# Scaling both halves of the recurrence's array, and splitting the streamed weights, on VectorE in place of GpSimd

## The chip, the cores and the metric

The kernel runs on one core of one Trainium2 chip. The metric is the device time of one execution in microseconds (us), lower is better. Five engines work side by side, each through its own queue in order: TensorE (PE in the rows; its weight loads are PEld), VectorE (DVE), ScalarE (ACT), GpSimd (POOL) and SyncE (SP), which issues nearly all DMAs. They wait for one another through semaphores.

## What is computed

One layer of a diffusion backbone on 1280 tokens: 1024 latent tokens and 256 prompt tokens, 1024 channels. It is a SwiGLU feed-forward (ffn1), a token-mixing step, and a second feed-forward (ffn2). All products have single-precision accuracy. Cut to the token mixing, which the change is about:

```python
proj = h @ p['w_mix_in']
hq, hi, hf_fwd, hf_bwd, hg, aq, ak, av = jnp.split(proj, idx, axis=-1)

def forget(hf):
    f = lb_h + (1.0 - lb_h) * jax.nn.sigmoid(heads(hf, DK_A).astype(jnp.float32))
    return jnp.log(f), 1.0 - f

lf_f, k_f = forget(hf_fwd)
lf_b, k_b = forget(hf_bwd)
o_f, s_f = hgrn_scan(q_rec, k_f, lf_f, i_rec, s0_f)
o_b, s_b = hgrn_scan(rev(q_rec), rev(k_b), rev(lf_b), rev(i_rec), s0_b)
o_rec = rms_norm(o_f + rev(o_b), p['hgrn_out_norm']).astype(h.dtype) * jax.nn.silu(heads(hg, DV_A))
...
o = jnp.concatenate([o_rec.reshape(B, T, -1), o_att.reshape(B, T, -1)], axis=-1) @ p['w_mix_out']
```

`hgrn_scan` is a gated linear recurrence of four heads, in both directions: the state is multiplied by f and gains k times v at each token; the output reads it with q.

## The kernel before

**Products in two parts.** A single-precision product is made of three reduced ones: each factor is split into a high part (a cast, tile name ending in h) and a low part (the factor minus its high part, ending in l), and `mm3` adds high×high, high×low and low×high. Activations are split once and stay in the on-chip memory (`hh`, `hl`). Weights come from HBM in pieces of 128x1024: `rload` (line 91) issues the DMA into a raw tile, `wload` (line 99) lets ACT cast the high part and one more engine subtract to get the low part. That engine is DVE while `self.half` is set, which is so in the prompt half of each feed-forward's first product, and POOL at all other times. `ahead(n)` keeps n pieces ready; four high and four low tiles go round. Pieces that POOL splits: the first two of ffn1, 32 of the input projection (`w_mix_in`), 24 of the output projection (`w_mix_out`), and the first three of ffn2, 61 in all.

**The recurrence of one head** (`hgrn`, from line 1060 on, with `hgrn_in` before it). All 1280 tokens stand in the free dimension. `A` holds k of both directions, `B` holds q times f of both, `P` (variable `pr`) the products of f over blocks. First `I` is the sum of A's two directions and a masked product (`sd`) fills the diagonal of the scores `s64`. Then come seven levels of doubling block size s: PE multiplies a rearranged copy of A (`I`, made by ACT) with B (40 small matmuls, tile `h0s` for head 0), DVE puts the result into `s64` under a mask (two `COPY_PREDICATED`), DVE multiplies one half of A (1280 columns) by block products, and B's two half arrays (640 columns each) are multiplied by block products in place: the one at offset 0 by DVE, the one at offset NT+s by POOL. POOL then makes the next level's `P` by multiplying neighbours. The next level's PE products need both halves of B and the new `I`.

**What runs beside it.** The generator of the recurrence is stepped by `tick` after every half of a projection's bank (24 matmuls of 256 columns), so PE alternates 24 projection matmuls with the 40 small ones of a level. The projection beside a head differs: head 0 and head 2 run the gate `hg` and a key or query projection, head 1 the values and keys, head 3 the second query group first. For the gate, POOL multiplies a 128x512 tile by the norm's gain (`hg<-hg,gam`) after each bank; for queries and keys DVE and POOL share the norm and the rotary embedding.

**Order.** Within an engine the order is not the source order: a scheduler at build time lists what is ready on its own clock, by program order among the ready. In the attention PE, DVE and ACT are pinned to the source order. At run time each queue is in order.

Of the kernel before, what the change touches and what calls it, by code (L numbers as in the profile page):

```python
# [9 lines left out]
F32 = mybir.dt.float32  # L10
# [3 lines left out]
ALU = mybir.AluOpType  # L14
# [8 lines left out]
NT = NS + NP  # L23
# [10 lines left out]
def sub(a, off, dims):  # L34
    return bass.AP(tensor=a.tensor, offset=a.offset + off,
                   ap=[list(a.ap[0])] + [list(d) for d in dims])


class Engine:


    def __init__(self, tc, eng):
        self.tc, self.eng, self.pinned = tc, eng, False
# [22 lines left out]
class Kern:  # L66
    def __init__(self, tc, ins, outs):
        self.tc, self.nc, self.i, self.o = tc, Engines(tc), ins, outs
        self.wq, self.wready, self.side = deque(), deque(), []
        self.h, self.hgen = [None] * 3, [None] * 3  # L70
        self.nw, self.nblk, self.half, self.tb = 0, 0, False, 7
        self.acc, self.nsq, self.ops, self.xt = [{}, {}, {}], [0] * 3, {}, [None] * 3
        self.late, self.lgen = deque(), None
        self.rawq, self.xraw, self.nraw, self.nr = deque(), None, 1, 0
# [24 lines left out]
    def wload(self):  # L99
        nc = self.nc  # L100
        if not self.rawq:
            self.rload()
        raw, name = self.rawq.popleft()
        shape = list(raw.shape)
        hi = self.wp.tile(shape, F32R, tag="wh", bufs=4, name=name + "h")
        nc.scalar.copy(hi, raw)
        lo = self.wp.tile(shape, F32R, tag="wl", bufs=4, name=name + "l")
        self.nw += 1
        eng = nc.vector if self.half else nc.gpsimd
        eng.tensor_tensor(lo, raw, hi.bitcast(F32), op=ALU.subtract)  # L110
        self.wready.append((hi, lo))
        while len(self.rawq) < self.nraw and self.wq:
            self.rload()
# [945 lines left out]
    def hgrn(self, ap, gp, hd, arrs):  # L1059
        nc = self.nc  # L1060
        A, B, q, pr = arrs
# [10 lines left out]
        def interleave(s):  # L1072
            I = gp.tile([P, NT], F32, tag="I", bufs=2, name=f"{n_}I{s}")
            nc.scalar.copy(I.rearrange("p (c r j) -> p c r j", r=2, j=s),
                           sub(A, 0, [(2 * s, NT // (2 * s)), (NT + s, 2), (1, s)]))
            return I

        def pairs(I, lv, move):


            banks = []
            for a, e in ((0, 8), (8, 10)):
                b = self.bank(f"{n_}s{lv}_{a}", (e - a) * 64)
                for t in range(a, e):
                    for h in range(2):
                        nc.tensor.matmul(b[64 * h:64 * h + 64, (t - a) * 64:(t - a + 1) * 64],
                                         I[:, t * P + 64 * h:t * P + 64 * h + 64], move(t * P, h), start=True, stop=True,
                                         tile_position=(0, 64 * h))
                banks.append((a, e, b.rearrange("p (a b) -> p a b", b=64)))
            return banks  # L1090
# [6 lines left out]
        s = 1  # L1097
        for lv in range(7):
            nb = NT // s
            C = nb // 2  # L1100
            if lv < 6:
                banks = pairs(I, s, lambda o, h: sub(B, o + 64 * h, [(2 * s, 32 // s), (NT + s, 2), (1, s)]))
            else:
                banks = pairs(I, s, lambda o, h: sub(B, o + (1 - h) * (NT + 64), [(1, 64)]))
            v_a = sub(A, 0, [(NT + s, 2), (2 * s, C), (1, s)])
            nc.vector.tensor_tensor(v_a, v_a, sub(pr, 1, [(nb - 1, 2), (2, C), (0, s)]), op=ALU.mult)
            if lv < 6:
                I = interleave(2 * s)
            for eng, off, po in ((nc.vector, 0, nb + 1), (nc.gpsimd, NT + s, 0)):
                v_b = sub(B, off, [(2 * s, C), (1, s)])  # L1110
                eng.tensor_tensor(v_b, v_b, sub(pr, po, [(2, C), (0, s)]), op=ALU.mult)
            for a, e, b in banks:
                if lv < 6:
                    nc.vector.copy_predicated(s64[:, a:e], self.mask[:, lv].unsqueeze(1).to_broadcast([P, e - a, 64]), b)
                else:
                    for h in range(2):
                        r = slice(64 * h, 64 * h + 64)
                        nc.scalar.copy(sc[r, a:e, 64 - 64 * h:128 - 64 * h], b[r])
            if lv == 6:
                for h in range(2):  # L1120
                    r = slice(64 * h, 64 * h + 64)
                    nc.scalar.copy(sc[r, :, 64 * h:64 * h + 64], s64[r])
            p2 = gp.tile([P, nb], F32, tag="P2" if lv % 2 == 0 else "P1", name=f"{n_}P{2 * s}")
            nc.gpsimd.tensor_tensor(p2, sub(pr, 0, [(2, nb)]), sub(pr, 1, [(2, nb)]), op=ALU.mult)
            pr = p2
            s *= 2
            if lv < 6:
                yield
# [387 lines left out]
def build(tc, ins, outs):  # L1516
    K = Kern(tc, ins, outs)
    nc = K.nc
# [11 lines left out]
    def ffn(st, name, which, hp, xp, side, nxt, done):  # L1530

        win, wout = ins[f"w_{name}_in"], ins[f"w_{name}_out"]
        pool = {}
        ai, pi = K.stream(K.in_blocks(win, name, lambda: pool["fp"]))
        ao, po = K.stream(K.out_blocks(wout, name, hp, xp, lambda: pool["op"]))
        ap_, pp = K.stream(K.prompt_out_blocks(wout, name, lambda: pool["op"]))

        def after():
            K.out_resident(hp, wout, name)
            ao(2)  # L1540
        K.half = True
        K.xraw, K.nraw = st["raw"](), 3
        K.prompt_in(st["t"], name)
        K.finish_all()
        K.half = False
        K.xraw, K.nraw = None, 1
        ai(1)
        st["close"]()
        with K.pool(name + "fp", side=side) as fp:
            pool["fp"] = fp  # L1550
            st["side"]()
            K.latents_in(fp, name, pi, after)
            K.finish_all()
        st["end"]()
        with K.pool(name + "op", side=side) as op:
            pool["op"] = op
            K.tb = 8
            m = 3 * which + 2
            K.latents_out(name, po, K.mt[m], K.ng[m], lambda c, d: done(op, c, d), lambda: ap_(2))
            K.prompt_out(name, pp, K.mt[m], lambda c, d: done(op, c, d))  # L1560
            nxt(op)

    with ExitStack() as top:
# [9 lines left out]
        with K.pool("xx", side="right") as xp:  # L1573
# [61 lines left out]
            def nxt(op):  # L1635
                mix_units()
                K.ahead(2)
                ap = pv.enter_context(K.pool("pv"))
                K.att_consts(cp, ap)
                K.proj_v(ap, 0)  # L1640
                K.finish_all()
                pv.close()
            ffn({"t": qp, "raw": lambda: qp, "close": q1.close, "side": lambda: K.side.append(adas()), "end": ta.close},
                "ffn1", 0, hp, xp, "right", nxt, done1)
        K.tb = 7
# [56 lines left out]
        with K.pool("xx2") as xp:  # L1702
# [29 lines left out]
            with K.pool("ps2", PSUM) as p:  # L1732
                K.ps = p, 8
                for c in (2, 1):
                    K.mix_out(c, range(8), done2)

                def done3(op, c, d):
                    K.nsq[c] += 1
                    if K.nsq[c] == 4:
                        K.nsq[c] = 0  # L1740
                        K.side.append(K.out_y(op, c, d // 4))
                ffn({"t": qp, "raw": lambda: hq["p"], "close": q1.close, "side": lambda: None, "end": lambda: None},
                    "ffn2", 2, hp, xp, None, lambda op: K.finish_all(), done3)
# [42 lines left out]
```

## Time and profile before

| | |
|---|---|
| median of 3 runs | 2743.75 us (2738.01, 2743.75, 2744.55) |
| the profiled execution | 2738.21 us, of which the span from first to last instruction is 2736.4 us |
| PE busy | 2658.0 us, 97% of the span |
| DVE busy | 1716.5 us, 63% |
| ACT busy | 1118.4 us, 41% |
| POOL busy | 861.5 us, 31% |
| mean granted TensorE clock | 0.991 of full speed |

In all profile rows times are microseconds from the span's start unless marked ns, `x` is a count of instructions, `out<-in` names the written and read tiles (buffer numbers left out), and `L49` is the line of a helper through which every operation is recorded. A timeline row is: start, duration, engine, line, operation, tiles, shape, count, and in brackets the idle time of that engine just before and what ended it. An instruction's duration runs from when its queue takes it up; a wait inside the engine counts as duration.

### The profile page before, as it was taken

How to read it: one execution, taken by the hardware profiler on the slowest of the kernel's cores; microseconds unless marked ns; L12 is line 12 of the kernel's file. 1: busy time of each engine (PE TensorE's matmuls, PEld its weight loads, DVE VectorE, ACT ScalarE, POOL GpSimd, SP SyncE). 2: the span in 40 equal slices, each digit the busy share in tenths (PEclk: the TensorE clock that was granted, in tenths of full speed). 3: DMA queues.
4: the chain of work that ended last, by engine and by line, in shares of the span. 5: the costliest groups of instructions: out<-in, count | busy, mean ns of one | idle time of the engine just before them, and what ended most of it. 6: DMA issues, size and time to landing. Idle time of an engine off the chain costs nothing.

```text
span 2736.4 us, 43768 instructions
## 1 busy us (share of the span) xinstructions
PE 2658.0 (97%) x17070; PEld 2330.0 (85%) x17070; DVE 1716.5 (63%) x2416; ACT 1118.4 (41%) x1896; POOL 861.5 (31%) x644
## 2 busy tenths in 40 slices
PE   7999999999998999999989899999999999999999
PEld 6987777888887989898989788888988888888889
DVE  4965454657978445555564588757855555658865
ACT  5732222323446423232322577735632333334444
POOL 1034444440002346556553121154034444420000
PEclk8999999999999999999999999999999999999999
DMA  9965665328645532232314845385743233358455
GB/s 313 275 181 185 191 191 185 101 97 304 211 138 182 171 97 78 86 100 67 95 57 144 194 106 119 137 267 166 210 137 110 91 108 105 107 173 291 137 179 191
DMA packets 412244, 429.29 MB, mean 157 GB/s; under 512 B 20620, under 2 KB 314756, under 8 KB 409988
## 3 DMA queue, kind: packets, MB, share of 16 engines
q1 hardware_dynamic: 411856, 426.43, 50.2%
q8 instruction: 134, 2.20, 0.3%
q14 instruction: 74, 0.61, 0.1%
q10 hardware_dynamic: 180, 0.06, 0.0%
HBM read 326.79 MB, written 99.61 MB: 156 GB/s over the span
## 4 chain that ended last, share of the span: by engine, by line
PE 58%; DVE 5%; POOL 2%; DMA 1%; issue 1%; ACT 0%; SPq 0%; POOLq 0%; DVEq 0%; ACTq 0%
PE ffn2po L49 8%; PE mob L49 4%; PE ffn2pp L49 2%; PE ffn2pg L49 2%; PE ffn2pu L49 2%; PE ffn1pp L49 1%; PE hi0b L49 1%; PE aq0b L49 1%; PE ak0b L49 1%; PE ak1b L49 1%; PE av1b L49 1%; PE hg1b L49 1%; PE hg0b L49 1%; PE hi1b L49 1%; PE ffn2u10p L49 1%
## 5 line engine op out<-in xcount | busy, mean ns | idle before, releaser
L49 POOL TENSOR_TENSOR nr<-nm,nh 128x4 f32<-128x4 f32 (+1 forms) x9 | 9.0, 1005 | 275.8 <-DVE nm L49 275.8
L49 PE MATMUL ffn1pp<-ffn1pvv,ffn1pw 128*128 128x256 f32 x528 | 65.5, 285 | 5.3 <-DVE ffn1pvv L49 5.3
L49 PEld LDWEIGHTS ffn1pp<-ffn1pvv,ffn1pw 128*128 128x128 f32 x528 | 63.9, 192 | 6.7 <-DVE ffn1pvv L49 6.1
L49 PE MATMUL ffn2pp<-ffn2pvv,ffn2pw 128*128 128x256 f32 x528 | 64.0, 283 | 0.0
L49 PEld LDWEIGHTS ffn2pp<-ffn2pvv,ffn2pw 128*128 128x128 f32 x528 | 63.6, 192 | 0.1
L49 DVE TENSOR_TENSOR sacc<-sacc,sq 128x512 f32<-128x512 f32 (+1 forms) x36 | 44.7, 1251 | 12.8 <-ACT sq L49 12.5
L49 POOL TENSOR_TENSOR hl<-nt,hh 128x256 fp32r<-128x256 f32 (+1 forms) x20 | 23.2, 1160 | 62.5 <-ACT hh L49 62.5
L49 POOL TENSOR_TENSOR ffn2w00a<-ffn2r,ffn2w00a 128x512 fp32r<-128x512 f32 x3 | 3.9, 1284 | 122.3 <-ACT ffn2w00a L49 122.3
L49 DVE TENSOR_TENSOR ffn1pw<-ffn1pw,ffn1pw 128x512 fp32r<-128x512 f32 x44 | 34.5, 813 | 7.9 <-ACT ffn1pw L49 7.9
L49 DVE TENSOR_TENSOR ffn2pw<-ffn2pw,ffn2pw 128x512 fp32r<-128x512 f32 x44 | 30.0, 690 | 13.7 <-ACT ffn2pw L49 12.1
L49 POOL TENSOR_TENSOR ffn1w00a<-ffn1r,ffn1w00a 128x512 fp32r<-128x512 f32 x3 | 3.9, 1292 | 107.3 <-ACT ffn1w00a L49 107.3
L49 ACT ACTIVATE nt<-nt,mt,sv 128x256 f32<-128x256 f32 (+1 forms) x40 | 25.8, 681 | 25.7 <-DVE sv L49 15.4
L49 ACT CAST ffn2pw<-ffn2pw 128x512 fp32r<-128x512 f32 x44 | 26.9, 619 | 16.0 <-PE ffn2pp L49 7.6
L49 ACT CAST ffn1pw<-ffn1pw 128x512 fp32r<-128x512 f32 x44 | 25.5, 616 | 14.8 <-DMA ffn1pw<-w_ffn_out 8.8
L49 PE MATMUL ada<-wada,cst 128*32 128x256 f32 x448 | 30.0, 385 | 0.0
L49 DVE TENSOR_REDUCE a_0mx<-a_0S 128x1 f32<-128x1536 f32 x8 | 14.1, 1757 | 24.6 <-DMA a0k<-k_d 13.2
L49 PEld LDWEIGHTS ada<-wada,cst 128*32 128x32 f32 x448 | 11.7, 109 | 14.7 <-issue 9.9
L49 PE MATMUL ffn1po<-ffn1w_10g,ffn1w_10b 128*128 128x512 f32 x84 | 20.6, 394 | 0.0
L49 PE MATMUL ffn2po<-ffn2w_4g,ffn2w_4b 128*128 128x512 f32 x84 | 20.4, 391 | 0.0
L49 PE MATMUL ffn2po<-ffn2w_5g,ffn2w_5b 128*128 128x512 f32 x84 | 20.4, 391 | 0.0
L49 PE MATMUL ffn1po<-ffn1w_8g,ffn1w_8b 128*128 128x512 f32 x84 | 20.3, 391 | 0.0
L49 PE MATMUL ffn2po<-ffn2w_6g,ffn2w_6b 128*128 128x512 f32 x84 | 20.3, 390 | 0.0
(4079 smaller groups left out, 9951.8 us busy)
## 6 DMA issues: line engine op xcount, KB each, us to landing
wada<-w_ada SPq DMA_DIRECT2D x112, 256.0 KB, 4.3
ffn1r<-w_ffn_in SPq DMA_DIRECT2D x44, 512.0 KB, 4.0
ffn2r<-w_ffn_in SPq DMA_DIRECT2D x44, 512.0 KB, 4.0
ffn1pw<-w_ffn_out SPq DMA_DIRECT2D x22, 512.0 KB, 3.4
ffn2pw<-w_ffn_out SPq DMA_DIRECT2D x22, 512.0 KB, 4.0
g_d<-ffn1t SPq DMA_DIRECT2D x33, 256.0 KB, 2.0
g_d<-ffn2t SPq DMA_DIRECT2D x33, 256.0 KB, 3.0
wadb<-w_ada SPq DMA_DIRECT2D x12, 512.0 KB, 8.8
```

The lines of the kernel that those rows point to most:

```text
L49: r = f(*a, **k)
```

## The change

Two edits. In `wload` the low part is always subtracted on DVE; the flag `half` and the counter `nw` go. In each of the seven levels of `hgrn` DVE multiplies both halves of B, one after the other; POOL keeps the product that makes the next `P`. No shape, buffer, load or matmul changes.

```diff
@@ -105,9 +105,7 @@
         hi = self.wp.tile(shape, F32R, tag="wh", bufs=4, name=name + "h")
         nc.scalar.copy(hi, raw)
         lo = self.wp.tile(shape, F32R, tag="wl", bufs=4, name=name + "l")
-        self.nw += 1
-        eng = nc.vector if self.half else nc.gpsimd
-        eng.tensor_tensor(lo, raw, hi.bitcast(F32), op=ALU.subtract)
+        nc.vector.tensor_tensor(lo, raw, hi.bitcast(F32), op=ALU.subtract)
         self.wready.append((hi, lo))
@@ -1106,9 +1104,9 @@
-            for eng, off, po in ((nc.vector, 0, nb + 1), (nc.gpsimd, NT + s, 0)):
+            for off, po in ((0, nb + 1), (NT + s, 0)):
                 v_b = sub(B, off, [(2 * s, C), (1, s)])
-                eng.tensor_tensor(v_b, v_b, sub(pr, po, [(2, C), (0, s)]), op=ALU.mult)
+                nc.vector.tensor_tensor(v_b, v_b, sub(pr, po, [(2, C), (0, s)]), op=ALU.mult)
@@ -1538,11 +1536,9 @@
-        K.half = True
         K.xraw, K.nraw = st["raw"](), 3
         K.prompt_in(st["t"], name)
         K.finish_all()
-        K.half = False
```

## Rows read from the trace of the kernel before

**Rows 1.** The page's first part: busy time of each engine, share of the span, instructions.

```profile
PE 2658.0 (97%) x17070; PEld 2330.0 (85%) x17070; DVE 1716.5 (63%) x2416; ACT 1118.4 (41%) x1896; POOL 861.5 (31%) x644
```

**Rows 2.** Who PE waited for between 952 and 1500 us, the four heads' stretch: us in total, times, longest.

```profile
PE h3s L49 <- DVE h3B L49: 6.1, 3, 2.7
PE h0s L49 <- POOL h0B L49: 2.5, 1, 2.5
PE h2s L49 <- POOL h2B L49: 2.5, 1, 2.5
PE h2sd L49 <- DVE h2I L49: 2.3, 1, 2.3
PE h0sd L49 <- DVE h0I L49: 2.3, 1, 2.3
PE h1sd L49 <- DVE h1I L49: 2.3, 1, 2.3
PE h3sd L49 <- DVE h3I L49: 2.3, 1, 2.3
```

**Rows 3.** Busy time in the stretch of head 1. Columns: stretch, length, busy (instructions) of PE, PEld, DVE, ACT, POOL, granted TensorE clock, DMA share, GB/s.

```profile
1088.10:1218.30 130.20, 127.88 (x1164) 120.26 (x1163) 72.41 (x103) 38.48 (x57) 67.88 (x44) 1.00 0.27 84
```

**Rows 4.** Timeline of PE: the first and the last of the seven levels' products in heads 0, 1, 2 and 3, and for head 1 the last but one (the first row is cut short by its window; its start counts).

```profile
1008.90 1.31 PE L49 MATMUL h0s<-h0B,h0I 128*64 128x64 f32 x26
1039.85 1.39 PE L49 MATMUL h0s<-h0B,h0I 128*64 128x64 f32 x40
...
1143.03 1.90 PE L49 MATMUL h1s<-h1B,h1I 128*64 128x64 f32 x40
1165.64 1.39 PE L49 MATMUL h1s<-h1B,h1I 128*64 128x64 f32 x40
1170.03 1.39 PE L49 MATMUL h1s<-h1B,h1I 128*64 128x64 f32 x40
...
1274.67 1.90 PE L49 MATMUL h2s<-h2B,h2I 128*64 128x64 f32 x40
1305.62 1.39 PE L49 MATMUL h2s<-h2B,h2I 128*64 128x64 f32 x40
...
1408.79 1.90 PE L49 MATMUL h3s<-h3B,h3I 128*64 128x64 f32 x40
1445.68 1.39 PE L49 MATMUL h3s<-h3B,h3I 128*64 128x64 f32 x40
```

**Rows 5.** Busy time in two stretches of 5 us, the columns as in Rows 3; the granted clock is the third number from the end.

```profile
1020.00:1025.00 5.00, 4.14 (x51) 4.02 (x52) 2.12 (x2) 0.73 (x1) 2.93 (x3) 0.66 0.01 3
1270.00:1275.00 5.00, 5.00 (x39) 4.75 (x37) 2.38 (x3) 3.05 (x2) 0.00 (x0) 0.66 0.17 56
```

**Rows 6.** Timeline of POOL in head 0: the gate's product, then B's second half, for which PE's wait in Rows 2 stands; last a gate's product beside no such product of DVE.

```profile
1016.15 1.88 POOL L49 TENSOR_TENSOR hg<-hg,gam 128x512 f32<-128x512 f32 x1
1018.00 2.81 POOL L49 TENSOR_TENSOR h0B<-h0B,h0P 128x640 f32<-128x640 f32 x1
...
1046.38 1.29 POOL L49 TENSOR_TENSOR hg<-hg,gam 128x512 f32<-128x512 f32 x1
```

**Rows 7.** Timelines of DVE (first five rows) and POOL (last two) in head 1's levels.

```profile
1153.73 0.74 DVE L49 COPY_PREDICATED h1s<-mask,h1s 128x512 f32<-128x512 uint8 x1
1154.36 0.81 DVE L49 TENSOR_TENSOR h1B<-h1B,h1P 128x640 f32<-128x640 f32 x1
1155.08 0.29 DVE L49 COPY_PREDICATED h1s<-mask,h1s 128x128 f32<-128x128 uint8 x1
1155.28 2.49 DVE L49 TENSOR_TENSOR h1A<-h1A,h1P 128x1280 f32<-128x1280 f32 x1
...
1160.51 1.48 DVE L49 TENSOR_TENSOR h1A<-h1A,h1P 128x1280 f32<-128x1280 f32 x1
...
1154.35 2.07 POOL L49 TENSOR_TENSOR h1B<-h1B,h1P 128x640 f32<-128x640 f32 x1
...
1167.12 1.28 POOL L49 TENSOR_TENSOR h1B<-h1B,h1P 128x640 f32<-128x640 f32 x1 [0.68 <-PE h1s L49]
```

**Rows 8.** Timelines of DVE (first two rows) and POOL (last two) before head 0's recurrence opens.

```profile
997.79 2.37 DVE L49 TENSOR_SCALAR h0P<-h0t,c,c 128x256 f32<-128x256 f32 x1 [1.80 <-ACT h0t L49]
...
1000.77 3.60 DVE L49 TENSOR_TENSOR h0I<-h0A 128x1280 f32<-128x1280 f32 x1
...
997.61 2.40 POOL L49 TENSOR_TENSOR k0w1l<-k0w1r,k0w1h 128x1024 fp32r<-128x1024 f32 x1 [2.15 <-ACT k0w1h L49]
...
1000.55 2.48 POOL L49 TENSOR_TENSOR h0P<-h0P 128x1280 f32<-128x1280 f32 x1
```

**Rows 9.** Timeline of DVE in ffn1's prompt half: a weight piece's low part on DVE.

```profile
45.63 1.22 DVE L49 TENSOR_TENSOR ffn1u1l<-ffn1u1r,ffn1u1h 128x1024 fp32r<-128x1024 f32 x1
```

**Rows 10.** Timelines of DVE and POOL in head 3, level 0: the rotary product, and B's second half.

```profile
1411.40 2.34 DVE L49 TENSOR_TENSOR aq_0y<-aq_0y,ropeFalse 128x512 f32<-128x512 f32 x1 [1.18 <-POOL aq_0t L49]
...
1411.34 1.85 POOL L49 TENSOR_TENSOR h3B<-h3B,h3P 128x640 f32<-128x640 f32 x1
```

**Rows 11.** Timelines of PE, DVE and POOL in the output projection: the norm of the prompt tokens.

```profile
1872.14 0.70 PE L49 MATMUL rb<-ndg,ones 128*128 128x256 f32 x2 [1.82 <-DVE ndg L49]
...
1869.51 2.58 DVE L49 TENSOR_TENSOR ndg<-ident,nr 128x256 f32<-128x256 f32 x1 [0.59 <-POOL nr L49]
...
1869.46 2.35 POOL L49 TENSOR_TENSOR mo_6l<-mo_6r,mo_6h 128x1024 fp32r<-128x1024 f32 x1
```

More of the change, by code (lines that the diff above doesn't have):

```diff
@@ L70, in __init__ @@
         self.h, self.hgen = [None] * 3, [None] * 3
-        self.nw, self.nblk, self.half, self.tb = 0, 0, False, 7
+        self.nblk, self.tb = 0, 7
         self.acc, self.nsq, self.ops, self.xt = [{}, {}, {}], [0] * 3, {}, [None] * 3
```

## The prediction

> **What bounds the kernel now.** I read the page's busy times first: PE is busy 97% of the span, DVE 63%, POOL 31% [rows 1]. So the time can only fall where PE stands idle (78.4 us in the whole span, 2736.4 less 2658.0) or runs at a lower clock, and it can rise only if new work comes between PE and its operands. Next I read who PE waits for in the four heads, where one of the two edits lies [rows 2]: 20.3 us in seven places, three kinds. Each head opens with a wait of 2.3 us for DVE's sum `I`; heads 0 and 2 wait once, 2.5 us, for POOL's half of B; head 3 waits three times for DVE's half. Then I compare the heads. From the first to the last level's products head 1 takes 27.00 us, heads 0 and 2 take 30.95 and head 3 takes 36.89 [rows 4]. Head 1 has no level wait and its clock is 1.00 throughout [rows 3], so 27.00 is the time that PE alone needs, 4.39 for a settled level (1165.64 to 1170.03). The excess of heads 0 and 2, 3.95 us each, is more than their 2.5 us wait: after it the granted clock reads 0.66 over 5 us, and so it does once after an opening wait, in head 2 [rows 5]. A wait thus costs its length and up to 1.4 us behind it (3.95 less 2.5).
>
> **Why DVE and POOL cost each other.** In head 1 POOL's half of B is taken up at 1154.35 while DVE works on its own half until 1155.08, and lasts 2.07; undisturbed it takes 1.28 [rows 7]. 1155.08 plus 1.28 is 1156.36, just its end of 1156.42. DVE's next product, on A, is taken up at 1155.28 and lasts 2.49; undisturbed it takes 1.48, or 1.40 to the next start, as rows run over by some 0.08 (0.81 for B, whose successor starts 0.72 later). 1156.42 plus 1.40 is 1157.82, its end (1157.77). So the two engines work on such products one after the other, whoever is first. The opening shows the same: DVE's `P` of 256 columns lasts 2.37 and ends when POOL's weight split does (997.61 plus 2.40 is 1000.01), and `I` lasts 3.60 as POOL's `P`, taken up 0.22 us earlier, ends at 1003.03 [rows 8]. [...]
>
> **The change part by part.**
>
> B's halves: 28 instructions (4 heads, 7 levels) leave POOL at 1.28 each and join DVE at 0.72 (start to start, 1154.36 to 1155.08) [rows 7]. Held one after the other, the pair of halves took 2.00 and takes 1.44. DVE's level becomes 0.63 (mask copy) + 0.72 + 0.72 + 0.20 (second copy) + 1.40 (A) = 3.67 us against PE's 4.39, so undisturbed it stays hidden, with 0.7 to spare. What can still cut in on POOL is `P` (small after two levels) and in heads 0 and 2 the gate's product, 1.29 us in every second level [rows 6], which brings the mean to 4.3.
>
> Heads 0 and 2: the 2.5 us wait arises because POOL takes the gate's product first (1016.15 to 1018.03) and only then B, which is held up to 2.81 [rows 6]. On DVE nothing queues B behind the gate. I replayed the levels by hand with the undisturbed durations and one holder at a time, from the end of level 0's products: the halves of level 1 end 7.5 us later, where PE wants them at 7.35, and once more, where the gate's product comes just ahead, PE waits 0.65. I take 0.9 us of waits left in each head: gain 3.95 − 0.9 = 3.05, twice, **6.1 us** (0 to 7.9).
>
> Head 1: no wait to win, 0.7 us spare a level: **0**; if the spare is eaten, up to 0.7 lost.
>
> Head 3: DVE is also the engine of the query norm, and waits for POOL inside that chain (1.18 before the rotary product); that product then lasts 2.34, where 0.6 is what I estimate for it undisturbed (0.72 times 512/640 columns), since POOL's half of B is taken up 0.06 us earlier [rows 10]. The change takes this holder away and adds 7 × 0.72 = 5.0 us to DVE's queue. In the replay the rotary product, one in two levels, gives back up to 1.7, and two levels pay 1.44; what remains is about 1 us at level 0, where nothing else delays B, and 1 over the rest. **2 us** (−5.0, if nothing is freed, to 9.9, head 1's length).
>
> The opening of each head: POOL's weight split of 2.40 stands just ahead of `P` on both engines [rows 8]. As 1.22 on DVE [rows 9] it ends near 998.83 in place of 1000.01, 1.2 earlier; POOL's own piece of A may still come ahead of DVE's `P`, so I take `P`, B and `I` 0.9 us earlier than now. PE's wait of 2.3 becomes 1.4: 4 × 0.9 = **3.6 us** (−1.2 a head if the split comes to stand between B and `I`, to 2.3 a head if `I` gets ahead of POOL's `P`: −4.8 to 9.2). The lower clock behind head 2's opening cost up to 0.34 × 5 = 1.7 [rows 5]; a shorter wait may not bring it on, I take **0.7** (0 to 1.7).
>
> The other weight pieces: 61 leave POOL at 2.40 and join DVE at 1.22 [rows 8, 9], 74 us for DVE in all. Where it has room they are hidden by the three pieces kept ahead: 24 matmuls between two levels take 4.39 − 1.39 = 3.0 us [rows 4], and a pair of pieces serves ten such, while DVE splits a piece in 1.22. In head 1's stretch DVE is busy 72 of 130 us [rows 3]. A split on DVE waits there for ACT's cast, and behind it queue the mask copies, B and A of the recurrence or, in the output projection, the residual add that frees PE's bank; PE waits only if that lasts longer than its spare. Three places show by themselves. The first product of ffn1 needs the first split, with nothing ahead of it to hide it; that is 2.40 − 1.22 = 1.2 shorter, which the loads of the start may take back: **0.5** (0 to 1.2). In the output projection the diagonal of the norm lasts 2.58, behind POOL's split of `mo_6`, and PE waits 1.82 [rows 11]: **1.0** (−1.2 to 1.8). Around the attention's start the first four pieces of the output projection are split, among the softmax's first blocks; there DVE's maxima would stand behind such a split: **−0.5** (−4 × 1.22 to 0).
>
> Sum: 6.1 + 0 + 2 + 3.6 + 0.7 + 0.5 + 1.0 − 0.5 = **13.4 us** gained. On the profiled execution that is 2738.2 − 13.4 = 2724.8. It is at the low end of the three runs; against the median, 2743.75, with which the new kernel's median is to be compared, it is **2730.4**. Nothing after the output projection is touched, and upstream gains pass down: the attention's first loads go into tiles (`hh0`, `hl0`) that the last projection reads, so they follow PE, not a fixed time.
>
> **The rivals.**
>
> (a) DVE becomes the bound of the levels. If the durations with interference stay as they are, because `P`, the gate and the rotary product go on cutting in, A keeps its 2.49 [rows 7] and a half of B may wait as well; a level is 0.63 + 2 × 0.72 + 0.20 + 2.49 = 4.8 with one such hold, 0.4 over PE's 4.39, and 0.8 more with two. The point of decision is 4.39. At 5.2 on the mean of the 21 levels of heads 0, 2 and 3, the loss is 21 × 0.8 = 17 us, less the 5 at the openings: 12 slower, 2756. For it: head 3 is held by DVE already [rows 2]. Against: the longest holder, POOL's own half, is what leaves.
>
> (b) The waits only move. The scheduler lists DVE anew; its order need not have B ahead of the mask copies or the weight split ahead of `P`. If PE then waits for DVE's second half where it waited for POOL's first, the openings' 3.6 and a bit of the levels are all there is, and half of that is lost to splits that stand waiting for ACT: gain 3, 2741.
>
> (c) Nearly all waits go: heads 0 to 3 all run as head 1 does (2 × 3.95 + 9.9) and the openings close (9.2 + 1.7): 29 us, 2715. Against: the gate's product and the query chain stay on POOL.
>
> (d) That the change does not do what it says is hardly open: POOL's instruction count must fall by 89 (61 and 28).
>
> **How the numbers follow.** The forecast, a gain of 9 to 19 around 13.4, has 0.48; (c), 19 to 29, 0.14; (b), from 8.2 faster to 8.2 slower, 0.27; (a) 0.11. 0.3%, about what a measurement of this kernel can tell from no change, is 8.2 us. So faster 0.62, same 0.27, slower 0.11. The range leaves out some 0.1 on each side: the upper part of (c) and (a): 2717 to 2746. The forecast's own range is 2725 to 2735.
>
> **What would show it.** POOL's busy time falls by 61 × 2.40 and at least 28 × 1.28, 182 us, to 680 or less; DVE's rises by 74 + 20 less the holds that vanish, so by less than 94. A in heads 0 to 2 lasts near 1.5 more often. PE's waits for POOL's B are gone, the opening waits are near 1.4, heads 0 and 2 take 28 us for their levels and head 3 about 35. I am wrong if head 1's levels take more than 27.5, if the opening waits are as long as before, or if PE waits for a weight's low part.

## The result and the profile after

The changed kernel takes 2717.69 us (median of four runs, 2716.61 to 2719.38) against 2744.15 (four runs, 2738.01 to 2747.15): a ratio of 0.9909, 95% interval 0.9893 to 0.9925. It is faster by 26.5 us; 13.4 were forecast, and the time lies 0.7 us inside the low end of the range (2717 to 2746), near rival (c) with its 2715. In a later comparison the kernel before had a median of 2740.43 and the changed kernel 2715.92, ratio 0.9912 (0.9897 to 0.9927): 24.5. The two profiled executions, 2738.21 and 2716.61 (span 2714.8), differ by 21.6, and the accounts below are made against that.

First the page's busy times, which answer to [rows 1].

```profile
PE 2650.1 (98%) x17070; PEld 2323.0 (86%) x17070; DVE 1724.1 (64%) x2505; ACT 1118.6 (41%) x1896; POOL 679.8 (25%) x555
```

POOL's count falls by 89 and its time by 181.7; DVE gets 89 instructions and only 7.6 us. By the undisturbed durations it was to get 94 (74 + 20): by that estimate the other 86 are what it had spent, held, in instructions that it already had.

Who PE waits for in the heads (940 to 1490 us; total, times, longest), against [rows 2]:

```profile
PE h3s L49 <- DVE h3B L49: 5.4, 4, 1.9
PE h0sd L49 <- DVE h0I L49: 0.8, 1, 0.8
PE h2sd L49 <- DVE h2I L49: 0.8, 1, 0.8
PE h3sd L49 <- DVE h3I L49: 0.8, 1, 0.8
PE h1sd L49 <- DVE h1I L49: 0.8, 1, 0.8
PE h3u L49 <- DMA h3v<-v_d: 0.6, 1, 0.6
```

Heads 0 and 2 no longer wait at any level; the four openings cost 0.8 in place of 2.3; head 3 still waits 5.4. In the kernel before, the same stretch has two more waits, which [rows 2] do not list:

```profile
PE h3u L49 <- ACT h3kt L49: 0.8, 1, 0.8
PE ck_0T L49 <- DMA ck<-cache_attn_k: 0.5, 1, 0.5
```

PE's timeline, the first and the last level's products of heads 0 to 3, against [rows 4]:

```profile
1007.76 1.90 PE L49 MATMUL h0s<-h0B,h0I 128*64 128x64 f32 x40
...
1034.64 1.39 PE L49 MATMUL h0s<-h0B,h0I 128*64 128x64 f32 x40
...
1136.39 1.90 PE L49 MATMUL h1s<-h1B,h1I 128*64 128x64 f32 x40
...
1163.27 1.39 PE L49 MATMUL h1s<-h1B,h1I 128*64 128x64 f32 x40
...
1265.01 1.90 PE L49 MATMUL h2s<-h2B,h2I 128*64 128x64 f32 x40
...
1291.89 1.39 PE L49 MATMUL h2s<-h2B,h2I 128*64 128x64 f32 x40
...
1393.64 1.56 PE L49 MATMUL h3s<-h3B,h3I 128*64 128x64 f32 x32
...
1427.91 1.39 PE L49 MATMUL h3s<-h3B,h3I 128*64 128x64 f32 x40
```

From start to start heads 0, 1 and 2 take 26.88 us each, head 3 34.27 (before: 30.95, 27.00, 30.95, 36.89). The stretches of the four heads, columns as in [rows 3]:

```profile
953.50:1082.70 129.20, 128.37 (x1171) 120.75 (x1169) 70.62 (x111) 38.49 (x57) 42.41 (x30) 1.00 0.29 91
1082.70:1211.30 128.60, 127.77 (x1165) 120.22 (x1163) 72.86 (x117) 38.08 (x57) 42.17 (x30) 1.00 0.27 85
1211.30:1339.90 128.60, 127.77 (x1164) 120.22 (x1163) 73.98 (x117) 38.23 (x57) 50.51 (x36) 1.00 0.29 89
1339.90:1451.30 111.40, 104.55 (x962) 96.50 (x960) 75.69 (x116) 33.74 (x49) 43.64 (x28) 1.00 0.28 89
```

The third number from the end is the granted clock: 1.00 in all four. Read in steps of 5 us, not one of the heads' stretches is below 0.95. Before, besides the two of [rows 5], three more were, one in head 2 (0.70 from 1285) and two in head 3:

```profile
1415.00:1420.00 5.00, 3.98 (x50) 3.89 (x51) 5.00 (x7) 1.26 (x1) 3.98 (x2) 0.67 0.02 3
1430.00:1435.00 5.00, 5.00 (x41) 4.93 (x37) 4.27 (x9) 1.74 (x2) 4.31 (x3) 0.66 0.16 56
```

So two sums explain the heads. Waits: 20.3 + 0.8 + 0.5 = 21.6 before, 9.2 after. Clock: (0.34 + 0.34 + 0.30 + 0.33 + 0.34) x 5 = 8.2 us before, none after; this counts each stretch as if PE had had work throughout, so it is an upper bound. 12.4 + 8.2 = 20.6, and the heads, counted from the first product of each head's first projection to the next's (head 3 to its output's first product), became shorter by 6.2, 1.6, 7.0 and 4.9, together 19.7.

Why the waits went is in DVE's instructions grouped by shape in the heads (count | total, mean ns | idle before). Kernel before:

```profile
L49 DVE TENSOR_TENSOR h0A<-h0A,h0P 128x1280 f32<-128x1280 f32 x7 | 13.2, 1885 | 1.3 <-ACT h0I L49 1.3
L49 DVE TENSOR_TENSOR h0B<-h0B,h0P 128x640 f32<-128x640 f32 x7 | 9.7, 1388 | 0.5 <-PE h0s L49 0.5
```

Changed kernel:

```profile
L49 DVE TENSOR_TENSOR h0B<-h0B,h0P 128x640 f32<-128x640 f32 x14 | 12.1, 906 | 0.7 <-PE h0s L49 0.7
L49 DVE TENSOR_TENSOR h0A<-h0A,h0P 128x1280 f32<-128x1280 f32 x7 | 10.4, 1484 | 1.3 <-ACT h0I L49 1.3
```

Twice as many halves of B, together with A, take 22.5 us, where half as many and A had taken 22.9. A is undisturbed in all seven levels. What POOL still does cuts in only beside B: in a level of head 0 where `P` and the gate come one behind the other (DVE first, then POOL) the two halves take 2.38 in place of 1.5, and still end at 1016.95, ahead of PE's next product of the head (1017.12).

```profile
1014.57 2.38 DVE L49 TENSOR_TENSOR h0B<-h0B,h0P 128x640 f32<-128x640 f32 x2
...
1017.06 1.48 DVE L49 TENSOR_TENSOR h0A<-h0A,h0P 128x1280 f32<-128x1280 f32 x1
...
1011.69 2.58 POOL L49 TENSOR_TENSOR h0P<-h0P 128x640 f32<-128x640 f32 x1 [6.99 <-DVE h0B L49]
1014.24 1.29 POOL L49 TENSOR_TENSOR hg<-hg,gam 128x512 f32<-128x512 f32 x1
```

The opening of head 0, DVE first, then POOL's `P`, against [rows 8]:

```profile
997.79 1.23 DVE L49 TENSOR_TENSOR k0w1l<-k0w1r,k0w1h 128x1024 fp32r<-128x1024 f32 x1 [1.51 <-ACT k0w1h L49]
998.93 0.41 DVE L49 TENSOR_SCALAR h0P<-h0t,c,c 128x256 f32<-128x256 f32 x1
999.64 3.60 DVE L49 TENSOR_TENSOR h0I<-h0A 128x1280 f32<-128x1280 f32 x1 [0.30 <-POOL h0A L49]
1003.16 0.41 DVE L49 TENSOR_TENSOR h0B<-h0q,h0P 128x256 f32<-128x256 f32 x1
...
999.58 2.32 POOL L49 TENSOR_TENSOR h0P<-h0P 128x1280 f32<-128x1280 f32 x1
```

DVE's `P` takes 0.41 in place of 2.37, and `I` now stands ahead of B's last piece. But `I` still takes 3.60: POOL's `P` is taken up 0.06 us ahead of it.

### The profile page after: what moved, and what is told of

The parts are those of the page before. It is cut to its first block, busy times and chain, and to the rows that moved or that the text cites. A ratio compares the mean times of both kernels' runs of the same rounds, so it can differ in the third digit from the quotient of the medians.

```text
span 2714.8 us, 43753 instructions
## 1 busy us (share of the span) xinstructions
PE 2650.1 (98%) x17070; PEld 2323.0 (86%) x17070; DVE 1724.1 (64%) x2505; ACT 1118.6 (41%) x1896; POOL 679.8 (25%) x555
## 4 chain that ended last, share of the span: by engine, by line
PE 88%; DVE 5%; DMA 2%; POOL 2%; issue 1%; ACT 1%; SPq 1%; ACTq 0%; POOLq 0%; DVEq 0%
PE ffn2po L49 8%; PE ffn1po L49 8%; PE mob L49 4%; PE ffn2pp L49 2%; PE ffn2pg L49 2%; PE ffn2pu L49 2%; PE ffn1pu L49 2%; PE ffn1pg L49 2%; PE ffn1pp L49 1%; PE hi0b L49 1%; PE ak0b L49 1%; PE aq0b L49 1%; PE ak1b L49 1%; PE av1b L49 1%; PE ada L49 1%
## 5 line engine op out<-in xcount | busy, mean ns | idle before, releaser
L49 DVE TENSOR_TENSOR sacc<-sacc,sq 128x512 f32<-128x512 f32 (+1 forms) x36 | 22.8, 643 | 2.6 <-ACT sq L49 2.3
L49 PE MATMUL ffn1po<-ffn1w_10g,ffn1w_10b 128*128 128x512 f32 x84 | 20.6, 394 | 0.0
L49 PE MATMUL ffn1po<-ffn1w_8g,ffn1w_8b 128*128 128x512 f32 x84 | 20.3, 390 | 0.0
```

The source lines that it names most:

```text
L49: r = f(*a, **k)
```

## The experiments

The theory on which the forecast rests: DVE and POOL work on such products one after the other, so the change shortens a shared hold. Its rivals: DVE is charged the moved work in full, or the waits only move. Eight kernels ran in two lots of four. In the first the kernel before has a median of 2740.56 (16 runs), in the second of 2740.43 (7 runs).

**The two edits apart.** `e1_halves_only` is the kernel before with only B's second half moved:

```diff
-            for eng, off, po in ((nc.vector, 0, nb + 1), (nc.gpsimd, NT + s, 0)):
+            for off, po in ((0, nb + 1), (NT + s, 0)):
-                eng.tensor_tensor(v_b, v_b, sub(pr, po, [(2, C), (0, s)]), op=ALU.mult)
+                nc.vector.tensor_tensor(v_b, v_b, sub(pr, po, [(2, C), (0, s)]), op=ALU.mult)
```

> Only B's second half moves to VectorE; the weights' low parts stay on GpSimd as in the kernel before. Theory 1 (one holder at a time of a path that both engines use; both edits shorten the holds): the level waits of heads 0 and 2 go with the lower clock behind them (3.95 us each, levels of 28.0 us first to last product), head 3 gains about 4, the four opening waits stay at 2.3 us as GpSimd's weight split still stands ahead of P; in all 10 to 14 us of the 22 between the two profiled executions. Rival (only the place in GpSimd's queue mattered): the same here, 10 to 14. Rival (the clock alone): the level waits may stay, the 0.66 stretches go.

Measured: 2728.46 (2724.86 to 2729.76), ratio 0.9956 (0.9942 to 0.9971), 12.1 us faster, as expected. PE's waits in the heads:

```profile
PE h3s L49 <- DVE h3B L49: 4.0, 3, 1.9
PE h0sd L49 <- DVE h0I L49: 2.3, 1, 2.3
PE h1sd L49 <- DVE h1I L49: 2.3, 1, 2.3
PE h2sd L49 <- DVE h2I L49: 2.3, 1, 2.3
PE h3sd L49 <- DVE h3I L49: 2.3, 1, 2.3
...
```

The levels of heads 0 to 2 run free with this edit alone (28.1, 28.0 and 28.1 us from the start of their first matmul to that of their last); the openings are as before. Between 950 and 1400 us the clock is low in one stretch of 5 us (0.66 from 1395), behind head 3's opening wait. There the lost time is given back: from the start of its first matmul to that of its last head 3's levels take 33.9 us, 35.5 in the changed kernel, and PE waits 4.0 for B in place of 5.4.

`e2_splits_only` is the kernel before with only the weights' low parts moved:

```diff
-        self.nw += 1
-        eng = nc.vector if self.half else nc.gpsimd
-        eng.tensor_tensor(lo, raw, hi.bitcast(F32), op=ALU.subtract)
+        nc.vector.tensor_tensor(lo, raw, hi.bitcast(F32), op=ALU.subtract)
```

> Only the weights' low parts move to VectorE; B's second half stays on GpSimd. Theory 1: opening waits fall from 2.3 to about 0.8 in all four heads (6 us, and head 2's lower clock behind it, 1.4), heads 0 and 2 keep a level wait near 2.5 for GpSimd's B, the output projection gains about 2: 8 to 11 us. Rival (only the queue place of B mattered): 0 to 2 us. The two single edits should add up to the whole, about 22 us between profiled executions, if they act at different places.

Measured: 2728.68 (2725.61 to 2729.93), ratio 0.9958 (0.9943 to 0.9972), 11.9 us faster, a little over the 8 to 11 expected. The waits in the heads:

```profile
PE h3s L49 <- DVE h3B L49: 6.3, 3, 2.9
PE h0s L49 <- POOL h0B L49: 2.5, 1, 2.5
PE h2s L49 <- POOL h2B L49: 2.5, 1, 2.5
...
PE h0sd L49 <- DVE h0I L49: 0.8, 1, 0.8
PE h3sd L49 <- DVE h3I L49: 0.8, 1, 0.8
PE h1sd L49 <- DVE h1I L49: 0.8, 1, 0.8
PE h2sd L49 <- DVE h2I L49: 0.8, 1, 0.8
```

The openings shrink and the levels stay, the mirror image of the first. The output projection too is this edit's: from its first product to that of ffn2 it takes 123.9 us here and in the changed kernel, 126.0 before and with the halves alone, where PE still waits 1.8 for the diagonal. 12.1 + 11.9 = 24.0, where the whole gained 26.5 and 24.5 in its own two comparisons: the edits add, and neither takes much from the other. Waits and clock account for the heads here too: for the halves alone, with that one low stretch, 7.2 + 6.5 = 13.7 us (13.1 measured); for the splits alone 5.9 of waits, which of the 8.9 measured leave 3.0 to the clock. That the edits add speaks against the rival that the waits only move.

**POOL's work put back, with nobody using it.** `e3_idle_product` is the changed kernel in which POOL multiplies B's first half once more, into a tile that is not in use yet, in levels 0 to 5:

```diff
+            if lv < 6:
+                nc.gpsimd.tensor_tensor(sub(sc, 0, [(s, C), (1, s)]), sub(B, 0, [(2 * s, C), (1, s)]),
+                                        sub(pr, nb + 1, [(2, C), (0, s)]), op=ALU.mult)
```

> The changed kernel, and in levels 0 to 5 of each head GpSimd multiplies B's first half once more into a tile that is unused then; nobody needs the result. Theory 1 (holds): VectorE's A and second half of B last up to 1.3 us longer in each level, a level needs 3.67 + 1.28 = 4.95 us of VectorE against 4.39 of TensorE, so heads 0 to 2 take 28.0 + about 3 each and the whole some 8 to 14 us more than the changed kernel. Rival (queue place): nobody waits for GpSimd's result, so the time stays within 2 us of the changed kernel.

Measured: 2732.81 (eight runs, 2731.44 to 2735.32), ratio 0.9975 (0.9965 to 0.9985): some two thirds of the gain are gone, by work on another engine that nobody waits for. That is 15 us above the changed kernel's 2717.69, where 8 to 14 were expected. DVE's products on A in head 0, and PE's waits in the heads:

```profile
L49 DVE TENSOR_TENSOR h0A<-h0A,h0P 128x1280 f32<-128x1280 f32 x7 | 16.8, 2400 | 1.3 <-ACT h0I L49 1.3
```

```profile
PE h3s L49 <- DVE h3B L49: 10.2, 5, 3.3
PE h0s L49 <- DVE h0B L49: 3.8, 5, 1.2
PE h2s L49 <- DVE h2B L49: 3.8, 5, 1.2
...
PE h1s L49 <- DVE h1B L49: 1.0, 4, 0.4
```

A goes from 1484 to 2400 ns; with engines that don't hold each other it would have stayed. The level passes PE's 4.39 above all in heads 0 and 2, where the gate is also on POOL, as rival (a) had it: the levels take 32.2, 29.5, 32.2 and 40.5 us, against 28.0, 28.0, 28.1 and 35.5 in the changed kernel. With the openings' 3.2 and 1.7 for a load PE waits 23.7 us in the heads, 14.5 more than in the changed kernel, and the heads are 15.9 longer. It is also more than the 21.6 of the kernel before, and yet the heads take 513.7 us in place of 517.5: the clock is 1.00 in every 5 us from 950 to 1400, through heads 0 to 2 and up to 4 us ahead of head 3's levels. If it is so in those as well, the account above gives +2.1 of waits and -8.2 of clock, -6.1, where -3.8 was measured; the 2.3 between are not explained.

`e4_idle_splits` is the changed kernel in which POOL subtracts once more, for the same 61 weight pieces, into the raw tile that is no longer needed:

```diff
+        if not self.half:
+            nc.gpsimd.tensor_tensor(raw, raw, hi.bitcast(F32), op=ALU.subtract)
```

> The changed kernel, and for the same 61 weight pieces GpSimd subtracts once more, into the raw tile that is dead by then. Theory 1 (holds): VectorE's P, B and I at the heads' openings are held again, the opening waits go from 0.8 back to 2 to 3.5 us (GpSimd's piece now starts 1.2 us later than it did), 5 to 10 us more than the changed kernel, and the residual adds of the output projection last longer. Rival (queue place): within 2 us, as no one reads what GpSimd writes; raw tiles come free 2.4 us later, which the three pieces ahead hide.

Measured: 2732.99 (nine runs, 2728.87 to 2734.29), ratio 0.9971 (0.9961 to 0.9981), 15 us slower than the changed kernel (5 to 10 were expected), but the loss is not at the openings, where it was expected: PE waits 0.9 there, not 2.3. DVE first, then POOL:

```profile
1005.09 3.68 DVE L49 TENSOR_TENSOR h0I<-h0A 128x1280 f32<-128x1280 f32 x1 [0.30 <-POOL h0A L49]
...
1005.02 2.40 POOL L49 TENSOR_TENSOR k0w1r<-k0w1r,k0w1h 128x1024 f32<-128x1024 f32 x1
1007.38 3.57 POOL L49 TENSOR_TENSOR h0P<-h0P 128x1280 f32<-128x1280 f32 x1
```

The idle split comes behind POOL's piece of A, not ahead of DVE's `P`, and it holds `I` for 2.2 us (3.68 less the 1.49 that `I` takes in the kernel without POOL's `P`, below), just as `P` does in the changed kernel; `P` itself is put off to where nobody wants it yet. So the opening depends on which of POOL's instructions is taken up beside `I`, and this kernel can't tell what the split at its old place costs (the kernel with the splits alone does: 1.5 an opening). In the profiled executions it loses 16.4: 5.4 before the first head, 1.8 in the heads, 3.5 in the attention, 4.3 in the output projection (a diagonal that PE waits 2.4 for; the clock is 0.66 over 5 us there, too), 1.4 behind it.

**What is left.** The second lot begins with `e8_changed_again`, the changed kernel itself as the mark.

> The changed kernel itself, on the same chip as these three, as the mark for them: 0.991 of the time of the kernel before, as in the first comparison; the same waits, 0.8 us at each opening and 5.4 in head 3.

Measured: 2715.92 (2715.58 to 2719.36), with the same waits. `e5_level0_p` takes the first `P` product from POOL as well:

```diff
-            nc.gpsimd.tensor_tensor(p2, sub(pr, 0, [(2, nb)]), sub(pr, 1, [(2, nb)]), op=ALU.mult)
+            (nc.gpsimd if lv else nc.vector).tensor_tensor(p2, sub(pr, 0, [(2, nb)]), sub(pr, 1, [(2, nb)]), op=ALU.mult)
```

> The changed kernel, with the first of the seven products that make the next P (128x1280, taken up by GpSimd at 999.58 for 2.32 us in head 0) given to VectorE as well; the output is the reference's. Theory, the two engines hold one another out: VectorE's sum I, which lasts 3.60 in the changed kernel, lasts about 1.4 once GpSimd does not hold it; if the P product comes behind I on VectorE it costs PE nothing at the opening and the four opening waits of 0.8 go: 3.2 us faster than the changed kernel, and no level wait, since P is read only after level 0's products. Rival, I is 3.6 long by itself (it reads both directions of A against each other): its length stays, and the opening waits stay at 0.8 or, if P is listed ahead of I, grow by P's 1.4 to 2.2. Second rival: the saved 0.8 is only handed on, because level 0's halves of B and A then stand behind P on VectorE: the openings close and the levels of each head grow by as much, so that the time is the changed kernel's.

Measured: 2712.89 (2712.72 to 2713.80), ratio 0.9899 (0.9884 to 0.9913), 3.0 us below the changed kernel; the two kernels' runs do not overlap. DVE's opening of head 0, and all that PE waits for in the heads up to 1480 us:

```profile
999.14 1.49 DVE L49 TENSOR_TENSOR h0I<-h0A 128x1280 f32<-128x1280 f32 x1 [0.30 <-POOL h0A L49]
...
1000.88 1.48 DVE L49 TENSOR_TENSOR h0P<-h0P 128x1280 f32<-128x1280 f32 x1
```

```profile
PE h3s L49 <- DVE h3B L49: 5.6, 4, 1.9
PE h3u L49 <- DMA h3v<-v_d: 0.5, 1, 0.5
```

`I` takes 1.49 once POOL is quiet, and the four waits are gone: 3.60 was 2.1 of hold, not the sum's own length. The levels do not grow (28.0, 28.0, 28.1 and 35.7 us, against 28.0, 28.0, 28.1 and 35.5): next to nothing is handed on. This is the fastest version that ran.

`e6_rotary_on_dve` moves POOL's last rotary product:

```diff
-                nc.gpsimd.tensor_tensor(t2.rearrange("p (t g e) -> p t g e", t=2, g=4), y4, rp[1], op=ALU.mult)
+                nc.vector.tensor_tensor(t2.rearrange("p (t g e) -> p t g e", t=2, g=4), y4, rp[1], op=ALU.mult)
```

> The changed kernel, with the one rotary product that GpSimd still makes for each group of queries and keys (tile t, 128x512) given to VectorE; the output is the reference's. Head 3's 5.4 us of waits for VectorE's B are what it is about. Theory, head 3 waits because VectorE's norm chain is held by GpSimd's product and by the handing to and fro: VectorE gains some 0.6 us of work a group and loses a hold of about as much and an idle time of 1.2; the waits shrink to 2 to 3 us, the kernel is 2 to 4 us faster than the changed one. Rival, head 3 waits because VectorE has too much to do in its levels (0.6 us more, five times): the waits grow to 7 to 8 us and the kernel is 2 to 3 us slower than the changed one.

Measured: 2718.14 (2715.60 to 2718.62), ratio 0.9915 (0.9901 to 0.9930): no gain over the changed kernel. Neither account holds. The waits for B fall from 5.4 to 4.0, less than the theory asked, but head 3's levels take 36.2 us in place of 35.5, with the clock at 0.66 from 1420 to 1425 in that execution (1.7 us), and its load is waited for 1.6 in place of 0.6.

`e7_both` has both moves.

> The changed kernel with both of these moves, the first P product and the rotary product on VectorE; the output is the reference's. If both theories hold the gains add: 5 to 7 us faster than the changed kernel. If VectorE's own work is what head 3 waits for, head 3's levels take 37 to 39 us in place of 35.5, and the kernel is within 2 us of the changed one.

Measured: 2713.53 (2712.41 to 2716.32), ratio 0.9899 (0.9882 to 0.9916): the first move's gain and nothing more, so the gains don't add because the second has none. Head 3's levels take 36.2 again, with 3.9 of waits for B.

What holds head 3 can be read from DVE's queue. In the changed kernel the work between its first product on A and its last (1393.58 to 1429.79) takes 36.2 us, and DVE stands idle in only 1.9 of them; PE's own work in head 3's levels is 34.27 less 5.4, 28.9. So the waits that are left are for DVE's own queue. No kernel ran that takes work off DVE there.

## Why the prediction was right, and where its sizes were off

The mechanism and the sign were right: B's second half and the splits are cheaper on DVE because POOL's longer instructions no longer hold it, shown by DVE's 7.6 us for 89 more instructions and, the other way round, by A at 2400 ns under an idle product. The sum, 13.4, was half of the 26.5 between the medians and 0.6 of the 21.6 between the profiled executions; the other 4.9 come from which executions were profiled, and no term answers to them. The time missed the forecast's own 2725 to 2735 and lies just inside the wider range, which owes as much to the room left for rival (c) as to the sum. By its terms, on the profiled executions:

| term | forecast | measured | from |
|---|---|---|---|
| levels of heads 0 and 2 | 6.1 | 8.1 | 30.95 to 26.88, twice |
| levels of head 1 | 0 | 0.1 | 27.00 to 26.88 |
| levels of head 3 | 2 | 2.6 | 36.89 to 34.27 |
| the four openings | 3.6 | 6.0 | 2.3 to 0.8 each |
| clock in head 2 beside the levels | 0.7 | 1.4 | 7.0 less 4.07 and 1.5 |
| heads 0 and 3, what is left | 0 | 1.4 | 6.2 and 4.9 less the above |
| start, up to the first head | 0.5 | -1.0 | first head's start 952.5 to 953.5 |
| head 3's output and attention | -0.5 | -0.1 | 298.5 to 298.6 |
| output projection | 1.0 | 2.1 | 126.0 to 123.9 |
| ffn2 | 0 | 0.9 | 841.9 to 841.0 |

They add up to 21.5 of the 21.6.

- **The 0.9 us left in heads 0 and 2 was wrong.** The replay let the gate's product come in once ahead of the halves and cost PE 0.65. On the chip it costs DVE 0.8 in such a level, and PE does not wait.
- **The openings' 0.9 was mis-sized**: 1.5. The forecast followed DVE's own chain, `P`, B and `I`, which was to start 1.2 earlier at most. In both kernels `I` is done 1.34 us after POOL's `P`, the holder (1003.03 and 1004.37 before, 1001.90 and 1003.24 after), and `P` gained more from the split's departure: counted from the head's first product it is taken up at 46.1 us (999.58 less 953.5) in place of 48.0 (1000.55 less 952.5).
- **The clock was the largest miss.** 2.9 us for a low clock behind the level waits of heads 0 and 2, and 0.7 for head 2's opening, were in the sum, none for head 3; the low stretches of the heads were worth up to 8.2 and all went. In head 3 the waits for B shrank by just 0.7, from 6.1 to 5.4, and the levels by 2.6.
- **The output projection** was taken at half its cover: the split `mo_6` left the diagonal alone entirely (0.42 in place of 2.58), and the whole wait of 1.82 went.
- **The start** gave nothing that can be told: PE's wait for the first pieces fell from 2.6 (1.6 for the low part, 1.0 for the high) to 0.8 (2.1 with the splits alone), but the first head starts at 952.2 to 954.9 in the kernels with the splits on DVE and no idle work added for POOL, and at 952.5 in the two without; the loads of the start scatter more than the term. A wait of PE for a weight's low part was named as a sign of being wrong; the one that is left, 0.8 for ffn1's first piece, is the 1.6 of before made shorter.
- **ffn2** was said to be untouched, though three of the 61 pieces are its own. Its 0.9 is no gain that can be told: from its first product to the end it takes 841.0 us here, 842.8 with the splits alone and 842.0 with the halves alone.
- **Two readings of the rows were off.** The heads held 21.6 us of waits, not 20.3. And DVE's `P` at the opening does not take its turn wholly behind POOL's split: it ends at 1000.16 (997.79 plus 2.37), 0.15 after the split, where it takes 0.41 alone. The other sums of that paragraph come out.
- **Place in the queue or hold.** For the 2.5 us in heads 0 and 2 the prediction named both, and no run has B ahead of the gate's product on POOL. The two took POOL 4.66 us there (1016.15 to 1020.81), undisturbed 1.29 and 1.28; by that estimate 2.1 of the 2.5 were hold.
- **Rival (a)** was the right mechanism with the wrong condition: the level does pass 4.39, as the idle product shows, but only with a POOL product of B's size in each. **Rival (b)** falls with the two edits apart. **Rival (c)**, 2715, came nearest to the time; against it stood that the gate and the query chain stay on POOL, and that counts in head 3 alone, which keeps 7.4 us over head 1's length, 5.4 of them waits and the rest more work of PE's own (two sets of query transposes among it).

That the two engines work one after the other is borne out by the idle product: in head 0 A becomes 0.92 us longer (2400 less 1484 ns) beside a POOL instruction whose result nobody uses.

## What to carry to other kernels

Before giving an idle engine part of a busy one's work, look whether the busy one's instructions become longer beside it: where two engines hold each other out, a product that takes 1.28 us on the one and 0.72 on the other costs the second less if it does both (in head 0, with the products on A, 22.5 us in place of 22.9). Count such holds from the mean duration of one shape at its disturbed and its undisturbed occurrences, and look for what is taken up just ahead of the instruction that PE waits for. Beside each wait of PE read the granted clock of the 5 us behind it: here the lost clock was worth up to 8.2 us beside 21.6 of waits. And before moving a product between engines in a stretch, see which engine sets its length: in head 3 that was DVE's own queue, and time that PE lost ahead of it came back in shorter waits (4.0 us with the halves alone, 5.4 in the changed kernel).

## What was not expected of the hardware

- The clock is not always low behind a wait of one length. With the halves alone, the openings' waits of 2.3 us leave the clock at 1.00 in heads 0, 1 and 2, and the same wait is followed by 0.66 in head 3; before, by 0.66 in head 2 alone. With the splits alone, the level wait of 2.5 is followed by 1.00 in head 0 (levels 30.6 us) and by 0.66 in head 2 (32.1); before, by 0.66 and 0.70 (32.1 each). With an idle product heads 0 to 2 have 11.0 us of waits, none longer than 1.2, and the clock is 1.00 throughout them. What decides stays open.
- A tiny instruction of POOL can last long: the power of 128x8 elements that makes the query norm's scale takes, in the changed kernel, 1.64 us for two of head 3's groups, 2.14 for two more and 4.28 for another. That one is taken up at 1424.87 beside DVE's product on A and ends at 1429.15, 1.6 us after the two halves of B that follow A (1427.57): it ended only behind three products of DVE in a row.
- The changed kernel's runs lie closer together: 2716.61 to 2719.38, against 2738.01 to 2747.15.
